# A hybrid decoder trunk on one core: the emission order recomputed from another table of durations, and some recurrent-branch operations moved to other engines

## The chip, the core and the metric

The program runs on one core of a Trainium2 chip. TensorE (PE in the profile) multiplies matrices into PSUM; VectorE (DVE), ScalarE (ACT) and GpSimd (POOL) work on tiles of 128 partitions; SyncE (SP), ACT and POOL issue transfers. Each engine runs its own instructions in program order and waits on semaphores of the others. The metric is the time of one execution on the device in microseconds; lower is better. The kernel before has a median of 2927.7 us over three runs, 2926.49 to 2927.87.

## The reference

Two layers over 512 tokens of width 1024, in float32. The middle part of a layer takes u = rmsnorm(x), one wide projection of u, and three branches that are gated, summed and projected back; a half-weighted SwiGLU stands ahead of it and behind it.

```python
for l in range(2):
    x = x + 0.5 * swiglu(rms_norm(x, ffn1_norm[l]), ...)      # 1024 -> 2 x 2816 -> 1024
    x = x + token_mixing(rms_norm(x, mix_norm[l]), ...)
    x = x + 0.5 * swiglu(rms_norm(x, ffn2_norm[l]), ...)
return rms_norm(x, final_norm)

# token_mixing, branch A (recurrent):
xa = causal_dwconv(rnn_x, conv_w) + conv_b                    # 4 taps
r, i = sigmoid(xa @ wa + ba), sigmoid(xa @ wx + bx)           # blocks of 64
log_a = -8 * r * softplus(-lam);  a = exp(log_a)
h = scan(a, sqrt(-expm1(2 * log_a)) * i * xa)                 # h_t = a_t h_{t-1} + u_t
ya = (h * gelu(rnn_g)) @ rnn_w_out
# branch B (short convolution):
yb = (c_b * causal_dwconv(c_c * c_h, sconv_w)) @ sconv_w_out  # 3 taps
# branch C: 8 heads attend, per query, to the 128 best keys of an indexer (8 heads of 64);
# merged = sum_b sigmoid(gate_b) * y_b ;  result = merged @ w_o
```

## The kernel before

Activations lie transposed: a tile is 128 channels by 512 tokens, so a vector of width 1024 is eight tiles (c or m from 0 to 7). Float32 accuracy comes from three products: every operand is cut into a high and a low part, and each product of a 128 by 128 weight tile with an activation tile is three matmuls of 512 columns (`mm3`, L528 to L530). I call these three one *tile product*; a *chunk* is the eight tile products that give one output tile in a PSUM bank of kind `psa`, of which there are three. Weights come in 512 KB pieces, one piece for eight tile products; in the middle part of a layer ACT makes high and negated low part (L378, L379) and a transfer that POOL issues adds the raw weight to the latter (L380). Three pairs of cut pieces are held.

What stands in which order on each engine is decided while the program is built. Each step of the computation is a Python generator that yields operations with a modelled cost (`PE`, `DVE`, `ACT`, `POOL` at L219 to L231). `Sched` plays them against a clock of its own: whenever an engine is free in the model, the ready operation of the lowest number is emitted to it (`_dispatch`). A step's number is its place in the program; `bump` makes evacuations of PSUM urgent (`EVAC`) and the top-k rounds of the indexer late (`TOPK_AT`). On the chip each engine then keeps exactly this order.

The change touches the middle part, `mix`. Its program in order of rank: v, indexer key and queries, k; then branch A. `a_x(c)` is the chunk x(c): DVE evacuates it into `xr` (L992), takes the first convolution tap (L994) and three more (L997); `cut` gives high part on ACT (L552) and low part on POOL (L556). `a_r(c)` makes two products of one tile each from it (ra, rx) with sigmoids on ACT (L1006, L1010). `a_scan` takes four channel tiles at a time: tanh, exp and square on ACT, two POOL operations in `em` (L1025, L1026), a square root on ACT, and in `fin` a multiply (L1036) and the scan (L1037) on DVE. `a_g(c)` is the gelu gate chunk g(c): evacuation (L1051), square on ACT, two POOL operations (L1054, L1055), tanh on ACT, two DVE operations (L1057 and, once the scan is there, L1059), and the cut into ya(c). Beside it `index(b)` scores the keys of query block b (L959 to L967) and finds the 128 best in 16 rounds of a maximum and a replacement (L971, L972; 48 rounds in a layer for the blocks of 256, 384 and 512 keys), with a threshold at the end (L974). `merge` then forms the sigmoid gates (chunks ga, evacuated at L1089) and the output projections of branch A (chunks wa(m), which need all eight ya). The attention heads q(h) follow, with `rope` (evacuation L855, shuffle L858, three POOL operations L859 to L861), then branch B, whose first tap is L1239, and w_o.

Of the kernel before, what the change touches and what calls it, by code (L numbers as in the profile page):

```python
# [15 lines left out]
AF = mybir.ActivationFunctionType  # L16
ALU = mybir.AluOpType
# [4 lines left out]
S = 512  # L22
# [99 lines left out]
class Sched:  # L122


    def __init__(self):
        self.t = 0.0
        self.n = 0
        self.heap = []
        self.free = {e: 0.0 for e in ("pe", "act", "dve", "pool", "sp")}
        self.ready = {e: [] for e in self.free}  # L130
        self.table = "sqrt"

    def _at(self, t, fn):
# [49 lines left out]
    def _dispatch(self):  # L183
        for eng, ready in self.ready.items():
# [17 lines left out]
            if s and self.table not in SETS[s]:  # L202
                self.table = SETS[s][0]
                cost += SWITCH
            op[3]()
            self.free[eng] = self.t + cost
# [14 lines left out]

def DVE(n, fn, fast=False, ap=0, **kw):
    return "dve", 0.07 + 0.06 * ap + n / (1920.0 if fast else 960.0), fn, kw


def ACT(n, fn, ap=0, **kw):
    return "act", 0.095 + 0.095 * ap + n / 1200.0, fn, kw


def POOL(n, fn, rate=0.0023, **kw):  # L230
    return "pool", 0.05 + n * rate, fn, kw  # L231

# [183 lines left out]
def trunk_kernel(ctx: ExitStack, tc: tile.TileContext, wall, wq, x_in, pos_in, cols_in, out):  # L416
# [37 lines left out]
    def col(name, l=0, j=0, c=0):  # L454
        i = col_of(name, l, j, c)
        return cols[:, i:i + 1]
# [408 lines left out]
    def mix(l, u, xs, nxt):  # L865
# [75 lines left out]
        def index(b, late):  # L941
# [27 lines left out]
            for rnd in range(TOPK // 8):  # L969
                m8 = sp.tile([P, 8], F32, name="m8", tag="m8", bufs=6)  # L970
                yield DVE(N, lambda: V.max(m8, acc[:, :N]), **bump)  # L971
                yield DVE(N, lambda: V.match_replace(out=acc[:, :N], in_to_replace=m8, in_values=acc[:, :N],  # L972
                                                     imm_value=-3e38), **bump)
            yield DVE(N, lambda: V.tensor_scalar(acc[:, :N], acc[:, :N], -2.9e38, NEG, op0=ALU.is_gt, op1=ALU.mult), True)  # L974
# [10 lines left out]
        def a_x(c):  # L985
# [7 lines left out]
            sch.release(banks["a"])  # L993
            yield DVE(S, lambda: V.tensor_scalar(y, xr[:, 0:S], col("rnn_conv_w", l, 0, c), col("rnn_conv_b", l, 0, c),  # L994
                                                 op0=ALU.mult, op1=ALU.add), True, ap=1)
            for j in range(1, 4):
# [18 lines left out]
        def a_scan(cs, pr):  # L1015
# [8 lines left out]
            def em(c, sq):  # L1024
                yield POOL(S, lambda: O.tensor_mul(sq, sq, th[c]))  # L1025
                yield POOL(S, lambda: O.tensor_add(th[c], th[c], sq))  # L1026

# [7 lines left out]
            def fin(c):  # L1035
                yield DVE(S, lambda: V.scalar_tensor_tensor(ix[c], th[c], 0.5, ix[c], op0=ALU.mult, op1=ALU.mult))  # L1036
                yield DVE(S, lambda: V.tensor_tensor_scan(th[c], rr[c], ix[c], 0.0, op0=ALU.mult, op1=ALU.add))  # L1037
                hs[c] = th[c]
                rr[c] = ix[c] = None
                sch.set(hev[c])  # L1040
# [6 lines left out]
        def a_g(c):  # L1047
# [5 lines left out]
            yield ACT(S, lambda: A.activation(t, g, AF.Square))  # L1053
            yield POOL(S, lambda: O.tensor_scalar(t, t, 0.044715 * GELU_C, GELU_C, op0=ALU.mult, op1=ALU.add), 0.00115)  # L1054
            yield POOL(S, lambda: O.tensor_mul(t, t, g))  # L1055
            yield ACT(S, lambda: A.activation(t, t, AF.Tanh), set="tanh")
            yield DVE(S, lambda: V.scalar_tensor_tensor(t, t, 1.0, g, op0=ALU.add, op1=ALU.mult))  # L1057
# [160 lines left out]
        def b_chunk(c):  # L1218
# [11 lines left out]
            def h_task():  # L1230
# [7 lines left out]
                y = box["y"] = G()  # L1238
                yield DVE(S, lambda: V.tensor_scalar(y, chb[:, 0:S], col("sconv_w", l, 0, c), None, op0=ALU.mult), True, ap=1)  # L1239
                for j in range(1, 3):  # L1240
# [187 lines left out]
```

## Time and profile before

| what | value |
|---|---|
| median of three runs | 2927.7 us |
| the profiled execution | 2929.0 us, its span 2927.3 us |
| TensorE busy in matmuls | 2857.4 us, 98% of the span |
| VectorE, ScalarE, GpSimd busy | 55%, 45%, 22% |
| mean granted TensorE clock | 0.987 |

The profile's page cuts the span into 40 slices of 73 us. VectorE stands at 9 tenths and more in two places, slices 7 and 8 (439 to 585 us, layer 0) and 27 and 28 (layer 1, 1448 us later), and the granted clock is at or above 9 tenths everywhere. The two places are branch A of each layer's middle part. A row of a windows view gives the busy time of each engine in a stretch, in brackets how many instructions reach into it, the mean granted clock, and the share of the transfer engines.

### The profile page before, as it was taken

The page shows a single profiled execution, that of the slowest core. Times are in us where ns is not written, and L with a number is a line of the kernel's source. Part 1 is how long each engine was busy: PE and PEld are TensorE (multiplying, and loading weights), DVE is VectorE, ACT ScalarE, POOL GpSimd, SP SyncE. Part 2 cuts the span into 40 slices and gives each one's busy share as a digit, 9 for nine tenths or more (in the row PEclk, how much of TensorE's full clock was granted, in tenths as well). Part 3 has the DMA queues.
Part 4 walks back from the last instruction along what each step waited for, and adds up shares of the span by engine and source line. Part 5 has one row for each costly group of instructions (what it writes and reads, how often), then busy time and mean ns, then how long its engine had stood idle before and what let it go on. Part 6 is the DMA issues. An engine that isn't in the chain of part 4 may idle for free.

```text
span 2927.3 us, 35856 instructions
## 1 busy us (share of the span) xinstructions
PE 2857.4 (98%) x14016; PEld 2384.6 (81%) x14016; DVE 1616.7 (55%) x2546; ACT 1319.5 (45%) x1817; POOL 638.5 (22%) x620
## 2 busy tenths in 40 slices
PE   8999998899999999999999999988999999999998
PEld 7888886678888888888888888866888888888887
DVE  7866659926312225666656666699171222256665
ACT  4333356647533453333433334566474334533333
POOL 1000064634222220000100001656242222300001
PEclk9999999899999999999999999999999999999999
DMA  4344486575688883344424444855846888733442
GB/s 165 106 115 112 134 188 143 136 165 136 140 189 187 190 189 94 105 116 114 129 85 112 114 111 141 192 136 133 180 119 152 197 185 186 180 85 114 112 117 63
DMA packets 118330, 407.47 MB, mean 139 GB/s; under 512 B 13137, under 2 KB 13777, under 8 KB 118161
## 3 DMA queue, kind: packets, MB, share of 16 engines
q1 hardware_dynamic: 77040, 263.23, 28.2%
q0 software_dynamic: 40400, 140.79, 27.5%
q8 instruction: 110, 1.80, 0.3%
q10 hardware_dynamic: 720, 1.17, 0.1%
q14 instruction: 60, 0.48, 0.1%
HBM read 281.40 MB, written 2.10 MB: 97 GB/s over the span
## 4 chain that ended last, share of the span: by engine, by line
PE 86%; DVE 11%; issue 1%; ACT 1%; DMA 0%; POOL 0%; SPq 0%; DVEq 0%; ACTq 0%; POOLq 0%
PE psa L530 23%; PE psa L529 23%; PE psa L528 23%; PE pst L722 2%; PE pst L719 2%; PE pst L721 2%; DVE g L972 2%; DVE m L971 2%; PE pso L721 1%; PE pso L722 1%; PE pso L719 1%; DVE g L997 1%; DVE g L965 1%; PE pss L719 1%; PE pss L722 1%
## 5 line engine op out<-in xcount | busy, mean ns | idle before, releaser
L528 PE MATMUL psa<-g,whi 128*128 128x512 f32 x3344 | 1332.6, 398 | 49.4 <-ACT g L552 17.2
L529 PE MATMUL psa<-g,whi 128*128 128x512 f32 x3344 | 1328.4, 397 | 4.6 <-POOL g L556 3.5
L530 PE MATMUL psa<-g,wlo 128*128 128x512 f32 x3344 | 1327.9, 397 | 1.2 <-DMA wlo<-wraw 1.2
L528 PEld LDWEIGHTS psa<-g,whi 128*128 128x128 f32 x3344 | 634.2, 190 | 194.8 <-issue 20.2
L530 PEld LDWEIGHTS psa<-g,wlo 128*128 128x128 f32 x3344 | 634.3, 190 | 151.3 <-DMA wlo<-wraw 2.1
L529 PEld LDWEIGHTS psa<-g,whi 128*128 128x128 f32 x3344 | 634.0, 190 | 146.7 <-POOL g L556 5.2
L384 ACT CAST whi<-wraw 128x768 fp32r<-128x768 f32 (+1 forms) x359 | 339.2, 950 | 764.3 <-PE pst L721 232.6
L378 ACT ACTIVATE wlo<-wraw 128x1024 fp32r<-128x1024 f32 x232 | 245.7, 1059 | 534.3 <-PE psa L530 526.5
L385 DVE TENSOR_TENSOR wlo<-wraw,whi 128x768 fp32r<-128x768 f32 (+1 forms) x359 | 391.6, 1101 | 31.8 <-ACT whi L384 27.1
L380 POOL DMA_DIRECT2D wlo<-wraw x232 | 201.3, 868 | 525.5 <-ACT wlo L378 498.7
L379 ACT CAST whi<-wraw 128x1024 fp32r<-128x1024 f32 x232 | 239.5, 1032 | 0.0
L722 PE MATMUL pst<-g,wlo 128*128 128x256 f32 x576 | 162.0, 281 | 0.6 <-DVE wlo L385 0.5
L721 PE MATMUL pst<-g,whi 128*128 128x256 f32 x576 | 161.7, 281 | 0.0
L719 PE MATMUL pst<-g,whi 128*128 128x256 f32 x576 | 161.6, 281 | 0.0
L317 POOL DMA_DIRECT2D wraw<-in_wq_dram x24 | 20.9, 872 | 625.9 <-DMA wraw<-in_wq_dram 469.9
L782 DVE SCALAR_TENSOR_TENSOR x<-pst,x 128x512 f32<-128x512 f32 x96 | 66.4, 692 | 149.0 <-PE pst L722 148.6
L336 POOL DMA_DIRECT2D wraw<-in_wq_dram x24 | 20.9, 871 | 548.6 <-DVE wlo L385 509.4
L719 PEld LDWEIGHTS pst<-g,whi 128*128 128x128 f32 x576 | 108.5, 188 | 4.3
L721 PEld LDWEIGHTS pst<-g,whi 128*128 128x128 f32 x576 | 108.4, 188 | 4.2
L722 PEld LDWEIGHTS pst<-g,wlo 128*128 128x128 f32 x576 | 108.6, 188 | 1.0 <-DVE wlo L385 1.0
L598 POOL TENSOR_TENSOR g<-g 128x512 f32<-128x512 f32 x44 | 61.0, 1387 | 216.6 <-ACT g L589 216.4
L1089 DVE TENSOR_TENSOR g<-psa,g 128x512 f32<-128x512 f32 x48 | 33.1, 689 | 133.7 <-PE psa L530 125.3
(219 smaller groups left out, 3167.1 us busy)
## 6 DMA issues: line engine op xcount, KB each, us to landing
wraw<-in_w_dram SPq DMA_DIRECT2D x423, 512.0 KB, 4.0
wlo<-wraw POOLq DMA_DIRECT2D x232, 512.0 KB, 5.6
wraw<-in_wq_dram SPq DMA_DIRECT2D x96, 384.0 KB, 3.0
wraw<-in_wq_dram POOLq DMA_DIRECT2D x48, 384.0 KB, 4.9
x<-in_x_dram SPq DMA_DIRECT2D x8, 256.0 KB, 4.4
out_dram<-g ACTq DMA_DIRECT2D x4, 256.0 KB, 3.0
out_dram<-g SPq DMA_DIRECT2D x4, 256.0 KB, 3.3
wraw<-in_w_dram SPq DMA_DIRECT2D x4, 128.0 KB, 4.2
```

The lines of the kernel that those rows point to most:

```text
L378: yield ACT(u.w, lambda: A.mul(u.lo, u.raw, -1.0))
L379: yield ACT(u.w, lambda: A.copy(u.hi, u.raw))
L380: yield "pool", 0.9, lambda: O.dma_start(u.lo, u.raw, accum_op=ALU.add), {}
L384: yield ACT(u.w, lambda: A.copy(u.hi, u.raw))
L385: yield DVE(u.w, lambda: V.tensor_sub(u.lo, u.raw, u.hi.bitcast(F32)), ap=1)
L528: T.matmul(ps, wh, xh, start=first, stop=False)
L529: T.matmul(ps, wh, xl, start=False, stop=False)
L530: T.matmul(ps, wl, xh, start=False, stop=last)
L719: T.matmul(o, u.hi[:, c], xh, start=begin and k == 0 and m == 0, stop=False, skip_group_check=True)
L721: T.matmul(o, u.hi[:, c], xl, start=False, stop=False, skip_group_check=True)
L722: T.matmul(o, u.lo[:, c], xh, start=False, stop=k == n - 1 and m == 1, skip_group_check=True)
L782: return DVE(S, lambda: V.scalar_tensor_tensor(dst, src, f, dst, op0=ALU.mult, op1=ALU.add), ap=1, **kw)
```

## The change

The model learns three things: an operation on DVE waits in the model for the POOL operation in progress (`port`; top-k rounds and PSUM evacuations are exempt, as are POOL operations of up to 8 elements), the top-k operations have a higher cost, and so has the scan. The computation changes in four places: `em` becomes one DVE operation, th * (sq + 1), in the place of two on POOL; the inner polynomial of gelu becomes one DVE operation in the place of two on POOL, its factor moved into the scale of the tanh; the first taps of both convolutions move from DVE to ACT. Lines behind L205 shift by 8 and less.

```diff
+        self.port = 0.0
...
+            if op[4].get("port"):
+                if eng == "dve":
+                    cost += max(0.0, self.port - self.t)
+                else:
+                    self.port = self.t + 0.85 * cost
...
 def DVE(n, fn, fast=False, ap=0, **kw):
+    kw.setdefault("port", "bump" not in kw)
...
 def POOL(n, fn, rate=0.0023, **kw):
+    kw["port"] = n > 8
...
-                yield DVE(N, lambda: V.max(m8, acc[:, :N]), **bump)
+                yield DVE(N, lambda: V.max(m8, acc[:, :N]), ap=2, **bump)
...
-                                                     imm_value=-3e38), **bump)
+                                                     imm_value=-3e38), ap=3, **bump)
...
-            yield DVE(S, lambda: V.tensor_scalar(y, xr[:, 0:S], col("rnn_conv_w", l, 0, c), col("rnn_conv_b", l, 0, c),
-                                                 op0=ALU.mult, op1=ALU.add), True, ap=1)
+            yield ACT(S, lambda: A.activation(y, xr[:, 0:S], AF.Identity, scale=col("rnn_conv_w", l, 0, c),
+                                              bias=col("rnn_conv_b", l, 0, c)), ap=1)
...
-                yield POOL(S, lambda: O.tensor_mul(sq, sq, th[c]))
-                yield POOL(S, lambda: O.tensor_add(th[c], th[c], sq))
+                yield DVE(S, lambda: V.scalar_tensor_tensor(th[c], sq, 1.0, th[c], op0=ALU.add, op1=ALU.mult))
...
-                yield DVE(S, lambda: V.tensor_tensor_scan(th[c], rr[c], ix[c], 0.0, op0=ALU.mult, op1=ALU.add))
+                yield DVE(S, lambda: V.tensor_tensor_scan(th[c], rr[c], ix[c], 0.0, op0=ALU.mult, op1=ALU.add), ap=9)
...
-            yield POOL(S, lambda: O.tensor_scalar(t, t, 0.044715 * GELU_C, GELU_C, op0=ALU.mult, op1=ALU.add), 0.00115)
-            yield POOL(S, lambda: O.tensor_mul(t, t, g))
-            yield ACT(S, lambda: A.activation(t, t, AF.Tanh), set="tanh")
+            yield DVE(S, lambda: V.scalar_tensor_tensor(t, t, 1.0 / 0.044715, g, op0=ALU.add, op1=ALU.mult))
+            yield ACT(S, lambda: A.activation(t, t, AF.Tanh, scale=0.044715 * GELU_C), set="tanh")
...
-                yield DVE(S, lambda: V.tensor_scalar(y, chb[:, 0:S], col("sconv_w", l, 0, c), None, op0=ALU.mult), True, ap=1)
+                yield ACT(S, lambda: A.activation(y, chb[:, 0:S], AF.Copy, scale=col("sconv_w", l, 0, c)), ap=1)
```

What this does to the order is seen at two places of layer 0. The first is VectorE at the end of branch A, before the change. `g_110` holds the scores of the block of 512 keys, L974 is its threshold, L1036, L1037 and L1059 end channel tiles 4 to 7 of the branch, L1089 evacuates gates.

```order
L971 MAX m8_4958<-g_110 128x8
L972 MATCH_REPLACE g_110<-m8_4958,g_110 128x512
L974 TENSOR_SCALAR g_110<-g_110 128x512
L1089 TENSOR_TENSOR g_4976<-psa_4922,g_3456 128x512
L1057 SCALAR_TENSOR_TENSOR g_4921<-g_4921,g_4920 128x512
L1089 TENSOR_TENSOR g_5022<-psa_4977,g_3456 128x512
L1036 SCALAR_TENSOR_TENSOR g_4613<-g_4851,g_4613 128x512
L1037 SCALAR_TENSOR_TENSOR g_4851<-g_4554,g_4613 128x512
L1059 TENSOR_TENSOR g_4715<-g_4715,g_4851 128x512
```

The same place after it; L1065 is the former L1059, L863 and L866 are the evacuation and shuffle of heads q0 and q1, L979 and L980 the former L971 and L972.

```order
L1065 TENSOR_TENSOR g_4722<-g_4722,g_4839 128x512
L1044 SCALAR_TENSOR_TENSOR g_4840<-g_4680,g_4741 128x512
L1044 SCALAR_TENSOR_TENSOR g_4841<-g_4762,g_4814 128x512
L1065 TENSOR_TENSOR g_4787<-g_4787,g_4840 128x512
L863 TENSOR_TENSOR g_5091<-psa_5049,g_3456 128x512
L1065 TENSOR_TENSOR g_4851<-g_4851,g_4841 128x512
L866 STREAM_SHUFFLE g_5092<-g_5091 32x512
L980 MATCH_REPLACE g_110<-m8_4991,g_110 128x512
L979 MAX m8_5126<-g_110 128x8
L980 MATCH_REPLACE g_110<-m8_5126,g_110 128x512
L979 MAX m8_5139<-g_110 128x8
```

Before, all 48 top-k rounds and the last threshold stand ahead of the last four L1059; now a replacement and 14 whole rounds over 512 keys, and that threshold, stand behind the last L1065, among the evacuations of wa(0) to wa(2). Between the chunk g(7) and the first tile product of wa(0) PE has 34 tile products before (gates ga(0) to ga(3) and two of q(0)) and 50 now (the same gates, q(0), q(1) and two of q(2)).

The second place is GpSimd ahead of the same four multiplies, before the change. L1025 and L1026 are `em` for tiles 4 to 7.

```order
L1055 TENSOR_TENSOR g_4921<-g_4921,g_4920 128x512
L1025 TENSOR_TENSOR g_4933<-g_4933,g_4851 128x512
L1025 TENSOR_TENSOR g_4972<-g_4972,g_4852 128x512
L380 DMA wlo_4982<-wraw_4617 128x1024
L1026 TENSOR_TENSOR g_4851<-g_4851,g_4933 128x512
L1026 TENSOR_TENSOR g_4852<-g_4852,g_4972 128x512
L1025 TENSOR_TENSOR g_4985<-g_4985,g_4853 128x512
L1025 TENSOR_TENSOR g_5012<-g_5012,g_4854 128x512
L1026 TENSOR_TENSOR g_4853<-g_4853,g_4985 128x512
```

And after it; L1020 is the former L1012, the product of gate and input for tile 7, L564 the cut of ya, L867 the first POOL operation of the rope of q(0).

```order
L1020 TENSOR_TENSOR g_4814<-g_4814,g_4586 128x512
L388 DMA wlo_4857<-wraw_4502 128x1024
L388 DMA wlo_4907<-wraw_4569 128x1024
L388 DMA wlo_4960<-wraw_4613 128x1024
L388 DMA wlo_5008<-wraw_4667 128x1024
L564 TENSOR_TENSOR g_5037<-g_4661,g_5036 128x512
L388 DMA wlo_5054<-wraw_4716 128x1024
L564 TENSOR_TENSOR g_5069<-g_4722,g_5068 128x512
L867 TENSOR_TENSOR g_5093<-g_5091,cq_88 32x512
```

The seven `em` operations that stood close together are gone from GpSimd, and the rope of a head now stands between two cuts of ya. Over the whole program ScalarE has 43 table loads in the new order and 35 in the old one; the eight more stand with the sigmoids of the gates and the exponentials of the heads. PE's order outside the middle parts of the layers is the same.

## Rows read from the trace of the kernel before

**Rows 1.** Head of the page: busy us, share of the span, instructions.
```profile
PE 2857.4 (98%) x14016; PEld 2384.6 (81%) x14016; DVE 1616.7 (55%) x2546; ACT 1319.5 (45%) x1817; POOL 638.5 (22%) x620
```
**Rows 2.** Who waited for whom, on PE: total us, times, longest.
```profile
PE psa L528 <- ACT g L552: 17.2, 4, 7.3
PE psa L528 <- DVE xr L992: 14.5, 4, 6.0
PE psa L528 <- DVE g L1089: 9.5, 4, 4.1
```
**Rows 3.** Windows of branch A, both layers: busy time of each engine.
```profile
core 0: us, PE busy (x) PEld busy (x) DVE busy (x) ACT busy (x) POOL busy (x), PEclk, DMA share, GB/s
482.00:500.00 18.00, 17.45 (x74) 13.82 (x74) 17.10 (x50) 12.62 (x18) 6.86 (x8) 1.00 0.58 147
500.00:536.00 36.00, 20.94 (x67) 15.36 (x68) 34.77 (x51) 23.13 (x30) 25.18 (x24) 0.81 0.53 132
536.00:580.00 44.00, 41.94 (x173) 32.93 (x171) 42.94 (x72) 33.83 (x46) 27.65 (x27) 0.96 0.60 132
580.00:602.00 22.00, 15.51 (x54) 11.43 (x55) 18.62 (x18) 11.77 (x17) 13.48 (x10) 0.89 0.57 138
602.00:662.00 60.00, 60.00 (x249) 48.34 (x249) 9.04 (x14) 23.80 (x27) 13.29 (x14) 0.96 0.81 179
...
1948.00:1984.00 36.00, 20.33 (x67) 15.11 (x68) 35.12 (x51) 23.30 (x30) 25.15 (x24) 0.80 0.55 131
```
**Rows 4.** A window of branch B, where PE never waits.
```profile
820.00:900.00 80.00, 80.00 (x345) 64.63 (x345) 17.74 (x26) 30.38 (x32) 19.94 (x24) 1.00 0.86 190
```
**Rows 5.** Groups of VectorE instructions, 482 to 602 us: busy us, mean ns.
```profile
L1036 DVE SCALAR_TENSOR_TENSOR g<-g 128x512 f32<-128x512 f32 x8 | 8.4, 1051 | 0.0
L1059 DVE TENSOR_TENSOR g<-g 128x512 f32<-128x512 f32 x8 | 8.4, 1050 | 0.1
L1057 DVE SCALAR_TENSOR_TENSOR g<-g 128x512 f32<-128x512 f32 x7 | 7.3, 1045 | 0.0
L994 DVE TENSOR_SCALAR g<-xr,cols 128x512 f32<-128x512 f32 x4 | 6.1, 1535 | 0.6 <-DVE xr L992 0.5
```
**Rows 6.** VectorE in order of time: start us, us.
```profile
571.55 1.72 DVE L1057 SCALAR_TENSOR_TENSOR g<-g 128x512 f32<-128x512 f32 x1
573.19 0.68 DVE L971 MAX8 m<-g 128x8 f32<-128x512 f32 x1
...
574.70 7.08 DVE L974 TENSOR_SCALAR g<-g 128x512 f32<-128x512 f32 x1
581.70 0.68 DVE L1089 TENSOR_TENSOR g<-psa,g 128x512 f32<-128x512 f32 x1
582.30 0.68 DVE L1057 SCALAR_TENSOR_TENSOR g<-g 128x512 f32<-128x512 f32 x1
```
**Rows 7.** GpSimd in the same stretch.
```profile
571.42 3.01 POOL L1025 TENSOR_TENSOR g<-g 128x512 f32<-128x512 f32 x2
...
575.01 2.81 POOL L1026 TENSOR_TENSOR g<-g 128x512 f32<-128x512 f32 x2
577.52 2.75 POOL L1025 TENSOR_TENSOR g<-g 128x512 f32<-128x512 f32 x2
579.99 1.50 POOL L1026 TENSOR_TENSOR g<-g 128x512 f32<-128x512 f32 x1
```
**Rows 8.** One line of VectorE over the run: ns least, median, most.
```profile
L997 DVE SCALAR_TENSOR_TENSOR g<-xr,cols,g x48: 721/752/1822, 435.3 to 1988.2; 128x512 f32<-128x512 f32 x48
```
**Rows 9.** Groups of ScalarE instructions, 482 to 602 us.
```profile
L1021 ACT ACTIVATE g<-g,spp 128x512 f32<-128x512 f32 x8 | 5.3, 709 | 0.0
L1032 ACT ACTIVATE g<-g 128x512 f32<-128x512 f32 x8 | 5.0, 624 | 0.1
L1044 ACT ACT_TABLE_LOAD x3 | 3.8, 1283 | 0.1
```

## The prediction

> **What bounds the kernel now.** I read the head of the page first. PE is in matmuls for 98% of the span, DVE for only 55% [rows 1], so nothing that merely relieves DVE on average is worth anything; what counts is where PE does not run at its full rate. The view of waits on PE names three large items: a tile that ACT cuts (L552), an evacuation of `xr` and one of a gate, 41.2 us in twelve waits over both layers [rows 2]. They lie in branch A, so I read that stretch by windows [rows 3], beside a window of branch B in which PE never waits [rows 4].
>
> A window tells what was lost as follows. In branch B 345 matmuls of 512 columns fill 80 us, 0.232 us each, 0.696 us for a tile product [rows 4]. From 482 to 662 us the five windows hold 74, 67, 173, 54 and 249 matmuls, which at that rate would cover 17.2, 15.5, 40.1, 12.5 and 57.7 us; the windows are 18, 36, 44, 22 and 60 us long. The losses are 0.8, 20.5, 3.9, 9.5 and 2.3 us, together 36.9 us [rows 3]. That is more than the idle time, since the granted clock falls to 0.81 and 0.89 behind the long waits, parts of these stretches being run at 1.2 GHz in the place of 2.4. Matmuls on a border are counted twice, so it is 1 or 2 us more. Layer 1 repeats it (36 us with 67 matmuls again), so 74 us in all are lost in the two branches A. With all of it back, the profiled execution would fall from 2929.0 to 2855 us. Start and end of the program stay as they are.
>
> In the same stretch DVE is busy for 17.10, 34.77, 42.94 and 18.62 of 120 us, 113.4 us [rows 3]. Between the chunk g(3) and the first of wa PE has 80 tile products of the branch and 34 of filler, 114, which take 79.3 us at the full rate. So DVE has 34.1 us more to do than PE there, and PE lost 36.9. It is DVE's stage, and I use the ratio 36.9 / 34.1 = 1.08 below for what an overhang of DVE costs with its lower clock.
>
> **The change part by part.** I add up what DVE must have done by the last multiply that ends a ya (L1059), from the 113.4 us, for layer 0.
>
> The deferred top-k. One round over 512 keys takes 1.51 us from the start of its maximum to the start of what follows (573.19 to 574.70) [rows 6]. A replacement and 14 rounds, 14.5 rounds, go behind the branch: 21.9 us less. They land in the stretch of wa, where DVE was busy for 9.04 of 60 us [rows 3]; the evacuations of wa stand among them, each at most one round late, and three PSUM banks give two chunks of 5.6 us to cover that. First user of the result is the softmax of the heads, which PE meets after more than ten chunks.
>
> The last threshold (L974). It took 7.08 us, from 574.70 to 581.78 [rows 6], while POOL ran one `em` operation after another until 581.49 [rows 7]; an ordinary DVE operation of 512 columns takes 0.68. The gate's evacuation behind it is one of the three waits of PE [rows 2]. It goes behind the branch with its rounds, and the `em` operations that held it up leave POOL: 7.1 us less.
>
> The first taps. Four L994 in the stretch took 6.1 us [rows 5]; they go. On ACT one costs 0.624 us without and 0.709 with one per-partition operand [rows 9], so 0.79 with two as an estimate; 0.62 and 0.90 are the bounds. That is 3.2 us more in 120 of which ACT is busy for 81 [rows 3]. The tap now waits on ACT for DVE's evacuation, and behind it in ACT's queue stand the cuts of the weight pieces; with three pieces held, of 5.6 us of PE each, 11 us cover that, and if the cover went, PE would wait for weights by as much as the evacuation is late. In branch B the tap leaves a DVE that is busy for 17.74 of 80 us for an ACT that is busy for 30.38, beside a PE that is busy throughout [rows 4]: nothing. Eight more table loads of 1.283 us [rows 9] are 10.3 us of ACT over the run, in stretches like 602 to 662, where it is busy for 23.80 of 60 [rows 3]: nothing.
>
> The operations that come from POOL. Eight for `em` and seven for gelu in this stretch. L1057 has the very form, two inputs of 512 columns from SBUF; undisturbed one such operation starts 0.60 us after the one ahead of it (581.70 to 582.30) [rows 6]. 15 times 0.60 is 9.0 us more.
>
> The waits on POOL. L1036, L1059 and L1057 average 1.05 us [rows 5] against 0.68 undisturbed [rows 6]: 0.37 times 23, 8.5 us of waiting. POOL's operations with two inputs in branch A go from 48 per layer (16 cuts, 8 products in L1012, 16 in `em`, 8 in gelu) to 24. I take half of the wait per instruction: 4.2 us less for these 23, and 15 times 0.185, 2.8 us, more for the new ones. The bounds for the new ones are no wait and 1.04 us each (the 1.72 of 571.55 less 0.68 [rows 6]), 0 and 15.6 us.
>
> Sum: 113.4 - 21.9 - 7.1 - 6.1 + 9.0 - 4.2 + 2.8 = 85.9 us. PE's filler ahead of wa grows by 16 tile products to 50, so that it has 130, 90.4 us. DVE now fits, with 4.5 us to spare. What stays lost I put at 5 us per layer: the 0.8 and 2.3 us of the two outer windows, and 2 us for waits of half a microsecond at single products, since the order is fixed and DVE's spare time is small. So 36.9 - 5 = 31.9 us per layer come back, 63.8 in all: 2929.0 - 63.8 = 2865.2 for the profiled execution. The median stands 1.3 us below that execution, so I say 2864.
>
> The Trainium skill (SBUF — State Buffer, "Who interferes with whom") says that a DVE operation in a two-port mode, or with two SBUF inputs, and a GpSimd operation take turns at a shared port, each for one whole instruction. The trace agrees for L1057 at 571.55, which took one POOL operation more than its own time, and not for L974, which outlasted five. By that rule the moved threshold would be worth the 1.5 us of one POOL operation and not 7.1 less its own time; the sum would be 5 us higher per layer for DVE, which the spare 4.5 us nearly hold, and the time 2866.
>
> **The rivals.** *The new operations wait.* Each of the 15 meets a POOL operation in progress and waits 1.04 us. For it: the means of L1036 and L1059 are half as long again as their own time, so about every third one waited that long [rows 5, 6]. Against it: POOL has half as many such operations, and 48 L997 have a median of 752 ns beside a least of 721 [rows 8]. DVE then has 85.9 + 15.6 - 2.8 = 98.7 us, 8.3 over PE; with the ratio 9.0, and with the 5 us of before 14.0 lost per layer. 2929.0 - 2 x 22.9 = 2883, a median of 2882. The Trainium skill (Perfetto Trace Analysis, "Optimizing Scalar/DVE Operations") speaks on this side: the two engines share a port, so that moving operations between them may not help.
>
> *Starving behind POOL (slower).* L974 shows that a DVE operation can stand behind a whole row of POOL operations, 6.4 us above 0.68 [rows 6, 7]. The ya cuts on POOL now have the rope of a head among them, and the DVE operations beside them are those that wa waits for. If such rows catch DVE often, each time costs 6.4 us. It decides from six times per layer: 85.9 + 6 x 6.4 = 124.3 is 34 us above PE's 90.4, the overhang of now. At eight times it is 137.1, 46.7 over, 50.4 lost with the ratio: 2929.0 + 2 x 13.5 = 2956, a median of 2955. Against it: the long wait was one threshold in each layer, none of the 48 L997 took over 1.82 us [rows 8], and the row of `em` that made it is gone.
>
> *It is not DVE's stage (no change).* PE could be waiting for weights, whose transfers POOL issues, and DVE's work be a coincidence; then 36.9 us stay lost and the median stays at 2928. For it: the transfer engines are at 0.81 and 0.86 when PE runs without waiting [rows 3, 4]. Against it: they are at 0.53 to 0.60 where PE waits, and the waits name ACT and DVE [rows 2].
>
> **How the numbers follow.** The forecast has 70%, with a range of its own from 2852 to 2878 (nothing lost, or 12 us per layer). The waiting operations have 17%, no change 5%, starving 7%; 1% is left for more than the counted loss coming back. A measurement of this kernel can tell about 0.2%, 6 us, from no change. Faster: 70 + 17 + 1 = 88%; same 5%; slower 7%. The range goes from 2850 (all of it back, with the matmuls on the borders) to 2896, which takes in the waiting operations up to 21 us lost per layer; outside lie no change, starving, and some 6% of the rest.
>
> **What would show it.** In windows of the same length from g(3) on, PE should hold some 155 matmuls in 36 us at a granted clock of 1.00, and DVE should be near 9 tenths of them. The last threshold should take under 3 us and start after the first evacuation of wa. L1043, L1065 and L1061 should average under 0.9 us; the waits of PE on L1095 and on `xr` L1000 should be below 2 us each per layer, and the wait of ra on ACT's cut below 2. Between 602 and 662 DVE should rise from 9 to above 30 us with PE still full. The prediction is wrong if the clock still falls below 0.95 in branch A, if wa still waits on ya by more than 5 us, or if PE waits for ACT's first tap or for weights.

## The result and the profile after

The changed kernel takes 2856.81 us (median of four runs, 2856.48 to 2857.57) against 2927.78 for the kernel before on the same chip (2926.49 to 2928.44). The ratio is 0.9758, with an interval from 0.9742 to 0.9775. The profiled execution took 2857.57 us; its mean granted clock is 0.997, against 0.987. The forecast was 2864, inside a range from 2850 to 2896.

The head of the page, which answers to [rows 1]:

```profile
span 2855.8 us, 35874 instructions
PE 2829.6 (99%) x14016; PEld 2371.4 (83%) x14016; DVE 1583.7 (55%) x2546; ACT 1347.6 (47%) x1857; POOL 562.4 (20%) x556
```

The number of matmuls is the same, and VectorE is as busy on average as before. Next the waits on PE, which answer to [rows 2] (what was waited for, us in total, times, longest):

```profile
PE psa L536 <- ACT whi L381: 5.3, 1, 5.3
PE psa L536 <- ACT g L1018: 2.8, 2, 1.4
PE pss L1157 <- DVE g L562: 2.2, 2, 1.2
...
PE psa L536 <- DVE xr L1000: 0.3, 2, 0.2
```

The first line is the start of the program, which nothing here touches. Of the three waits that cost 41.2 us, the one on `xr` is left with 0.3 us, and the ones on ACT's cut (L552, now L560) and on the gate's evacuation are gone. One product of the branch now waits 1.4 us in each layer for a sigmoid on ACT (L1018). Windows of branch A, as in [rows 3]; the last one lies in branch A of layer 1:

```profile
480.56:570.63 90.07, 88.52 (x380) 70.99 (x379) 87.45 (x153) 78.04 (x105) 35.67 (x34) 1.00 0.77 178
500.00:536.00 36.00, 34.45 (x148) 27.27 (x147) 35.62 (x47) 28.77 (x41) 23.94 (x20) 1.00 0.77 173
580.00:602.00 22.00, 20.78 (x97) 17.11 (x96) 19.86 (x53) 13.70 (x23) 6.08 (x6) 1.00 0.80 181
602.00:662.00 60.00, 60.00 (x278) 49.36 (x277) 17.68 (x45) 35.27 (x52) 12.81 (x13) 1.00 0.77 178
1930.00:1966.00 36.00, 34.62 (x149) 27.95 (x150) 35.13 (x69) 29.28 (x42) 15.06 (x14) 1.00 0.75 174
```

In 36 us there are now 148 matmuls (layer 1: 149) where 67 stood in either layer, and the granted clock is 1.00 where it was 0.81 and 0.80. (The page of the kernel before has 8 tenths in slice 8, which holds most of that stretch; that the clock stood at 9 tenths and more everywhere, as said above, was not so.) The first row runs from the start of g(3) to the end of the last multiply that ends a ya. DVE is busy for 87.45 us of it; the chunk of wa(0) starts at 573.20, so PE took 92.6 us from g(3) to it. DVE's rows for the same stretch answer to [rows 5] (busy us, mean ns of one, idle before them):

```profile
L979 DVE MAX8 m<-g 128x8 f32<-128x384 f32 (+2 forms) x26 | 13.7, 526 | 0.4
L1005 DVE SCALAR_TENSOR_TENSOR g<-xr,cols,g 128x512 f32<-128x512 f32 x12 | 13.4, 1113 | 0.5 <-ACT g L1002 0.2
L1044 DVE TENSOR_TENSOR_SCAN g<-g 128x512 f32<-128x512 f32 x8 | 12.6, 1593 | 0.0
L1043 DVE SCALAR_TENSOR_TENSOR g<-g 128x512 f32<-128x512 f32 x8 | 6.4, 811 | 0.6 <-ACT g L1051 0.6
L1065 DVE TENSOR_TENSOR g<-g 128x512 f32<-128x512 f32 x8 | 6.4, 806 | 0.0
L1033 DVE SCALAR_TENSOR_TENSOR g<-g 128x512 f32<-128x512 f32 x8 | 5.4, 686 | 0.3 <-ACT g L1039 0.2
L1063 DVE SCALAR_TENSOR_TENSOR g<-g 128x512 f32<-128x512 f32 x7 | 5.4, 770 | 0.0
L1061 DVE SCALAR_TENSOR_TENSOR g<-g 128x512 f32<-128x512 f32 x6 | 5.2, 874 | 0.0
```

L1033 and L1061 are the operations that came from POOL. The three products that averaged 1.05 us are at 0.77 to 0.81 us; but the later taps and the scan, which no term of the sum names, have become dearer: between 480 and 600 us the kernel before has `L997 ... x12 | 9.9, 824` and `L1037 ... x8 | 9.8, 1220`, against 1113 and 1593 ns here.

Where the time came from can be told more closely. For each kernel I take a window's length less the columns of the matmuls that start in it at the full rate (0.2323 us for 512 columns); what is left is lost. The second column group shows the evacuation of x(4), the first chunk for the second half of the recurrent channels, and when its last tap ended (us from the span's start, layer 0). Each ratio is to runs of the kernel before on the same chip at the same time (medians of 2926.4 to 2927.8 us), so differences of a few us between two kernels are to be read with the intervals.

| kernel | median, us | ratio to before (interval) | lost 500–540 | lost 540–620 | x(4): evacuated, taps end |
|---|---|---|---|---|---|
| before | 2927.8 | – | 21.9 | 14.7 | 505.4, 510.1 |
| order by the new costs, old operations (e1) | 2886.7 | 0.9861 (0.9845–0.9878) | 11.2 | 9.1 | 493.8, 504.9 |
| new operations, old costs (e2) | 2894.2 | 0.9886 (0.9871–0.9901) | 12.6 | 8.1 | 499.7, 505.0 |
| cost of top-k alone (e3) | 2906.6 | 0.993 (0.991–0.995) | 17.9 | 9.7 | 498.1, 504.1 |
| the port alone (e4) | 2898.7 | 0.9903 (0.9883–0.9923) | 15.6 | 9.0 | 498.5, 507.6 |
| threshold with two inputs (e5) | 2924.8 | 0.9991 (0.998–1.0002) | 22.1 | 14.3 | – |
| half the top-k rounds (e9) | 2897.6 | 0.9897 (0.9868–0.9925) | 14.7 | 8.4 | 491.0, 499.1 |
| order by new costs, late `em` (e13) | 2893.1 | 0.9885 (0.9867–0.9903) | 7.7 | 14.1 | 494.2, 497.9 |
| the change | 2856.8 | 0.9758 (0.9742–0.9775) | 1.9 | 1.6 | 491.9, 497.0 |
| the change, maximum twice (e10) | 2901.4 | 0.991 (0.9881–0.9938) | 10.7 | 14.5 | 498.8, 504.0 |
| the change, first taps on DVE (e7) | 2861.2 | 0.9772 (0.9744–0.9801) | 6.1 | 0.5 | 490.4, 494.1 |
| the change, gelu on POOL (e8) | 2861.5 | 0.9777 (0.9759–0.9795) | 2.1 | 4.7 | 491.4, 496.7 |
| the change, `em` on POOL (e11) | 2869.3 | 0.9803 (0.9785–0.9821) | 4.7 | 7.5 | 494.7, 500.6 |
| the change, dearer taps (e12) | 2852.4 | 0.9745 (0.9732–0.9758) | 2.6 | 0.3 | 490.6, 495.9 |

### The profile page after: what moved, and what is told of

Read it like the earlier page. It is cut to its first block, busy times and chain, and to the rows that moved or that the text cites. A ratio compares the mean times of both kernels' runs of the same rounds, so it can differ in the third digit from the quotient of the medians.

```text
span 2855.8 us, 35874 instructions
## 1 busy us (share of the span) xinstructions
PE 2829.6 (99%) x14016; PEld 2371.4 (83%) x14016; DVE 1583.7 (55%) x2546; ACT 1347.6 (47%) x1857; POOL 562.4 (20%) x556
## 4 chain that ended last, share of the span: by engine, by line
PE 91%; DVE 6%; ACT 2%; issue 1%; DMA 0%; SPq 0%; DVEq 0%; ACTq 0%
PE psa L536 24%; PE psa L538 24%; PE psa L537 24%; PE pst L730 2%; PE pst L727 2%; PE pst L729 2%; PE pso L727 1%; PE pso L730 1%; PE pso L729 1%; DVE g L1044 1%; DVE g L1005 1%; DVE g L980 1%; PE pst L1187 1%; PE pss L727 1%; PE pss L729 1%
## 5 line engine op out<-in xcount | busy, mean ns | idle before, releaser
L388 POOL DMA_DIRECT2D wlo<-wraw x232 | 200.8, 866 | 569.1 <-ACT wlo L386 549.7
L767 DVE TENSOR_TENSOR g<-psa,g 128x512 f32<-128x512 f32 x88 | 60.8, 691 | 77.4 <-PE psa L538 77.3
```

What stands on the lines that cost most here:

```text
L388: yield "pool", 0.9, lambda: O.dma_start(u.lo, u.raw, accum_op=ALU.add), {}
```

## The experiments

Three theories stood at the start. The balance (T1): DVE's work up to the last ya against PE's products, whatever the order. The order (T2): the new order does it, the operations do nothing. The port (T3): the operations that leave POOL do it by relieving DVE of waits.

**Order alone and operations alone.** e1 has the changed costs and the old operations (the port's factor is 0.6; its order comes out of the model with the old operations, so it is not the change's order row by row). e2 has the new operations and the old costs.

```diff
 e1:
+                    self.port = self.t + 0.6 * cost
+                yield DVE(N, lambda: V.max(m8, acc[:, :N]), ap=2, **bump)
...
+                yield DVE(S, lambda: V.tensor_tensor_scan(...), ap=9)
 e2:
+            yield ACT(S, lambda: A.activation(y, xr[:, 0:S], AF.Identity, ...), ap=1)
+                yield DVE(S, lambda: V.scalar_tensor_tensor(th[c], sq, 1.0, th[c], op0=ALU.add, op1=ALU.mult))
+            yield DVE(S, lambda: V.scalar_tensor_tensor(t, t, 1.0 / 0.044715, g, op0=ALU.add, op1=ALU.mult))
```

> The model's new costs alone (port, top-k, scan), operations as before; the port factor is 0.6 in the place of 0.85. Its order puts 10.5 top-k rounds and the last threshold behind the last ya and gives PE 50 tile products of filler. Theory 1 (what counts is DVE's work ahead of the last ya against PE's products): DVE 113.4 - 15.9 - 7.1 = 90.4 us against 90.4 of PE, about 5 us lost per layer, 2864. Theory 2 (the order alone counts, being nearer to what the chip does): the same, 2857 to 2864. Theory 3 (the work taken off GpSimd frees the shared port, the order hardly matters): most of the loss stays, 2905 to 2925.

> The moved operations alone, under the old costs. No top-k round goes behind the last ya, filler 42 products. Theory 1: DVE 113.4 - 6.1 (taps) - 6.4 (threshold no longer behind em) + 9.0 - 4.2 + 2.8 = 108.5 us against 122 products, 84.9 us; 23.6 over, times 1.08 is 25.5 lost per layer, 2905. Theory 2: near 2925. Theory 3: 2857 to 2870.

Measured: 2886.7 and 2894.2 us, so 41 and 34 us of the 71; together a little more than the whole. T2 and T3 alone fall. T1 missed both: it expected 2864 of e1, nearly all of the gain, and 2905 of e2. In e1 PE waits at xr:

```profile
PE psa L536 <- DVE xr L1000: 13.9, 4, 6.1
```

DVE in that stretch of e1 (start us, us, instruction):

```profile
493.84 0.68 DVE L1000 TENSOR_TENSOR xr<-psa,g 128x512 f32<-128x512 f32 x1
494.63 7.42 DVE L1002 TENSOR_SCALAR g<-xr,cols 128x512 f32<-128x512 f32 x1
502.08 0.75 DVE L1005 SCALAR_TENSOR_TENSOR g<-xr,cols,g 128x512 f32<-128x512 f32 x1
```

and POOL beside it (L1033 and L1034 are `em` in e1, L388 issues a transfer):

```profile
494.56 0.86 POOL L388 DMA_DIRECT2D wlo<-wraw  x1
495.18 2.81 POOL L1034 TENSOR_TENSOR g<-g 128x512 f32<-128x512 f32 x2
...
497.72 2.80 POOL L1033 TENSOR_TENSOR g<-g 128x512 f32<-128x512 f32 x2
500.22 1.53 POOL L1034 TENSOR_TENSOR g<-g 128x512 f32<-128x512 f32 x1
501.45 1.13 POOL L388 DMA_DIRECT2D wlo<-wraw  x1
```

The first tap of x(4) stands 7.42 us in DVE, until the row of five `em` operations is through: what befell the threshold in the kernel before [rows 6, 7] befalls a tap here. It is earlier in branch A and so delays ra(4) to ra(7) and all behind them. From this came a fourth theory, that of the *nearer deadline*: not DVE's sum up to the last ya decides, but when the chunks x(4) to x(7) are evacuated and convolved. The runs below support it in part; none moves the evacuation of x(4) and nothing else. In the kernel before, the last matmul of x(4) is this one on PE:

```profile
493.17 0.39 PE L530 MATMUL psa<-g,wlo 128*128 128x512 f32 x1
```

and DVE comes to its evacuation (L992) 11.8 us later, since the old order has 25 top-k rounds ahead of it:

```profile
504.94 0.54 DVE L972 MATCH_REPLACE8 g<-m,g 128x384 f32<-128x384 f32 x1
505.40 0.68 DVE L992 TENSOR_TENSOR xr<-psa,g 128x512 f32<-128x512 f32 x1
506.19 1.04 DVE L994 TENSOR_SCALAR g<-xr,cols 128x512 f32<-128x512 f32 x1
```

The change has 15 ahead of it, and the chunk, which ends at 491.9, is evacuated at once; its three later taps end at 497.0:

```profile
491.95 0.68 DVE L1000 TENSOR_TENSOR xr<-psa,g 128x512 f32<-128x512 f32 x1
492.55 0.68 DVE L1033 SCALAR_TENSOR_TENSOR g<-g 128x512 f32<-128x512 f32 x1
...
494.67 2.33 DVE L1005 SCALAR_TENSOR_TENSOR g<-xr,cols,g 128x512 f32<-128x512 f32 x3 [0.24 <-ACT g L1002]
```

**The parts of the costs.** e3 has the dearer top-k and nothing else of the change, e4 the port and nothing else.

```diff
 e3:
+                yield DVE(N, lambda: V.max(m8, acc[:, :N]), ap=2, **bump)
+                yield DVE(N, lambda: V.match_replace(...), ap=3, **bump)
 e4:
+                    cost += max(0.0, self.port - self.t)
+                else:
+                    self.port = self.t + 0.85 * cost
```

> Only the higher modelled cost of the top-k operations. 5 rounds and the threshold go behind the last ya, filler 42. Theory 1: 113.4 - 7.6 - 7.1 = 98.7 us against 84.9, 13.8 over, 14.9 lost per layer, 2884. Theory 2: between 2870 and 2890, as the largest error of the model is mended. Theory 3: no change, 2920 or more.

> Only the modelled port. 1.5 rounds and the threshold go behind the last ya, filler 50. Theory 1: 113.4 - 2.3 - 7.1 = 104.0 us against 90.4, 13.6 over, 14.7 lost per layer, 2883. Theory 2: between 2880 and 2905. Theory 3: no change, 2920 or more.

2906.6 and 2898.7: each helps by 21 and 29 us, less than the balance gives for the rounds that they defer (2884 and 2883). The order alone (T2) had 2870 to 2890 and 2880 to 2905, so only e4 lies in its range. In both, x(4) is evacuated near 498, later than in e1.

**What kind of operation waits.** In e5 the last threshold of layer 0 is a two-input operation in the place of L974.

```diff
+                yield DVE(N, lambda: V.scalar_tensor_tensor(acc[:, :N], acc[:, :N], -2.9e38, neg1.to_broadcast([P, N]),
+                                                            op0=ALU.is_gt, op1=ALU.mult), True)
```

> The kernel before, with the three top-k thresholds of layer 0 as a scalar_tensor_tensor with a broadcast second input from SBUF, in the place of a tensor_scalar; layer 1 unchanged, as a control; order and instruction count the same. If the long wait belongs to the kind of operation (a tensor_scalar cannot get in between two GpSimd operations, one with two inputs can), the last threshold of layer 0 takes at most 2.4 us, layer 1's still 7, PE's wait for the gate shrinks from 4.1 to under 1 us in layer 0, and the time falls by 4 to 6 us to 2922 to 2924. If any DVE operation would stand behind the whole row, it takes 6 to 7 us in both layers and the time stays at 2928.

```profile
573.50 7.35 DVE L977 SCALAR_TENSOR_TENSOR g<-g,neg 128x512 f32<-128x512 f32 x1
```

By the first answer it would have taken at most 2.4 us, and it took 7.35: of these two forms of a DVE operation neither is spared the long wait. The time didn't move beyond the noise (0.998 to 1.0002).

**Less and more top-k.** e9 is the kernel before with every second top-k round left out; e10 is the change with each maximum taken twice.

```diff
 e9:
+                yield DVE(N, lambda: rnd % 2 or V.max(m8, acc[:, :N]), **bump)
+                yield DVE(N, lambda: rnd % 2 or V.match_replace(out=acc[:, :N], ...), **bump)
 e10:
+                yield DVE(N, lambda: (V.max(m8, acc[:, :N]), V.max(m8, acc[:, :N])), ap=2, **bump)
```

> The kernel before with every second top-k round left out (24 of 48 per layer, so that 64 and not 128 keys are chosen), the order of everything else as before. Theory 1: 53 us of rounds in the stretch from g(3) on become 26.5, DVE 86.9 us against 79.3 of PE, 7.6 over, 8.2 lost per layer and 2 to 5 of small waits, 2870 to 2876. Theory 2 (the order must be mended): 2905 or more. Theory 3 (the port): 2905 or more, since no operation with two inputs goes.

> The changed kernel with the maximum of every top-k round done twice on DVE, which the model doesn't know of; order and result the same. From g(3) to the last ya that is 25.5 more maxima, 14 us (8 x 0.46, 16 x 0.58, 1.5 x 0.71). Theory 1: DVE's 90 us become 104 against PE's 92.6 in that stretch, 11.5 over, about 12 lost per layer, 2880 to 2884. If DVE had more to spare than the sum says, 2860 to 2870; if each late operation is paid by PE in full (17 us with the 8 maxima ahead of g(3)), 2890 or more.

By the balance, e9 has so much taken from DVE that 10 to 13 us per layer should stay lost (2870 to 2876). It took 2897.6, under the 2905 of the other two theories as well, and still waits for `xr`:

```profile
PE psa L528 <- DVE xr L992: 16.3, 4, 4.2
```

There x(4) is evacuated on time, at 491.0, but its taps end only 8 us later, two of them taking 5.06 us together from 492.77 on, while POOL ran `em`. That is the strongest evidence against the balance alone: the work is gone and the time is not back. In e10 the order is the change's but the rounds ahead of x(4) last longer, and its evacuation falls to 498.8; it gives back 44.6 of the 71 us. That is the third answer of the expectation (2890 or more) and not the 2880 to 2884 of the balance, and at 22 us per layer it is more than the 17 us of maxima that were added.

**Each operation by itself, in the change.** The factor of the port is another one in two of them (0.9 in e7, 0.8 in e11), so a part of the difference can be the order's.

```diff
 e7:
+            yield DVE(S, lambda: V.tensor_scalar(y, xr[:, 0:S], col("rnn_conv_w", l, 0, c), ...), True, ap=1)
 e8:
+            yield POOL(S, lambda: O.tensor_scalar(t, t, 0.044715 * GELU_C, GELU_C, op0=ALU.mult, op1=ALU.add), 0.00115)
+            yield POOL(S, lambda: O.tensor_mul(t, t, g))
 e11:
+                yield POOL(S, lambda: O.tensor_mul(sq, sq, th[c]))
+                yield POOL(S, lambda: O.tensor_add(th[c], th[c], sq))
```

> The changed kernel with the first tap of the recurrent branch back on DVE (four in the stretch), known to the model; its port factor is 0.9 in the place of 0.85. 14.5 rounds and the threshold still behind the last ya, filler 50. By the term of the sum (6.1 us): DVE 96 against 92.6, 3.7 lost per layer, 2864. If the taps' waits were owed to em on GpSimd, which is gone: 4 x 0.55 = 2.2 us more, 2857 to 2859.

> The changed kernel with gelu's two operations back on GpSimd, known to the model. 12 rounds behind the last ya, 17 top-k rounds ahead of the evacuation of x(4). The runs so far say that two things are lost in x(4) to x(7): evacuations that stand behind too many rounds, and taps on DVE that wait for em on GpSimd. Gelu's operations stand beside the g chunks and not there: 2858 to 2864. If any operation with two inputs on GpSimd costs alike, they are half of what came off it: 2872 or more.

> The changed kernel with em's two operations back on GpSimd, known to the model (port factor 0.8). 13.5 rounds behind the last ya, 16.5 ahead of x(4). If em beside the taps of x(4) to x(7) is the costly meeting: the taps of x(4) or x(5) end 4 to 6 us later than in the changed kernel, 6 to 10 us more are lost per layer between 500 and 540 us, 2868 to 2878. If all operations on GpSimd cost alike: the same as with gelu there, within 4 us.

2861.2, 2861.5 and 2869.3: over the change's 2856.8 the taps of branch A on ACT make 4.4 us, gelu 4.7 and `em` 12.5. The intervals of the first two ratios overlap that of the change, so that neither is shown to be worth anything; that of `em` doesn't (from 0.9785 up, against 0.9775 at most). So `em` is the one part of the three that counts clear of noise, though it puts work on DVE. The taps came out between their two answers, and gelu in the first of its own. e11 lies in the range of its first answer (2868 to 2878), but not by the meeting named there: the taps of x(4) end 3.6 us later and not 4 to 6, and of what is lost beside the change 2.8 us lie between 500 and 540, where 6 to 10 were expected, and 5.9 behind that.

**Out of the taps' way.** e13 is e1 with `em` of the first four tiles held until x(7) is convolved, so that no row of `em` can meet a tap of x(4) to x(7); factor 0.5.

```diff
+                if c < 4:
+                    yield xa[7].ev
```

> The model's new costs alone with the old operations (port factor 0.5), and em of the tiles 0 to 3 made to wait until x(7) is cut. 20 rounds ahead of x(4), 3 rounds and no less behind the last ya. If em beside the taps is what the new order alone could not mend: at most 5 us lost between 500 and 540 us, against 11.2 with em in its place, and the tap of x(4) ends within 6 us of its evacuation; the whole 2868 to 2882, since the later em now meets the rounds. If the place of em is of no account: 10 us or more still lost there, 2884 or more.

Half of it came true. The taps of x(4) end 3.7 us after its evacuation (11 in e1), and the loss from 500 to 540 falls from 11.2 to 7.7 us, where at most 5 were expected. But the total is 2893.1, above e1 and above the expected 2868 to 2882, in the range of the other answer (2884 or more). The row of `em` met another victim, the threshold of 384 keys on DVE:

```profile
526.18 9.07 DVE L982 TENSOR_SCALAR g<-g 128x384 f32<-128x384 f32 x1
```

while POOL ran `em` (L1035 and L1036 in e13) without a pause:

```profile
525.76 0.88 POOL L388 DMA_DIRECT2D wlo<-wraw  x1 [0.35 <-ACT wlo L386]
526.37 1.59 POOL L1035 TENSOR_TENSOR g<-g 128x512 f32<-128x512 f32 x1
527.61 4.04 POOL L1036 TENSOR_TENSOR g<-g 128x512 f32<-128x512 f32 x3
531.31 1.16 POOL L388 DMA_DIRECT2D wlo<-wraw  x1
531.92 1.88 POOL L1036 TENSOR_TENSOR g<-g 128x512 f32<-128x512 f32 x1
533.17 1.85 POOL L1020 TENSOR_TENSOR g<-g 128x512 f32<-128x512 f32 x1
```

PE's largest wait in e13 is then one for DVE:

```profile
PE psa L536 <- DVE g L1061: 7.5, 2, 3.8
```

In layer 0 it lasts from 535.1 to 538.8; the threshold ends at 535.25, and two rounds stand between it and that evacuation. That the one makes the other is read from the times and was not tried by itself. The taps of x(4) are one victim of the rows among several: the change takes the row off POOL, while moving it in time moved the damage.

**Dearer taps in the costs.** Since a tap takes 752 ns in the median (1113 on average in the stretch above, waits included) and the model gives it about 0.66 us (0.07 + 0.06 + 512/960), e12 raises their cost in the change, with the port's factor at 0.7.

```diff
+                    self.port = self.t + 0.7 * cost
...
+                                                            op0=ALU.mult, op1=ALU.add), ap=2)
```

> The changed kernel with a modelled cost of the taps on DVE of 0.72 in the place of 0.66 us (the trace has 0.74), port factor 0.7: an attempt on the rest, 1.4 us of wait at ra(6) and 1.2 at a head per layer. If a nearer table still helps, 2850 to 2855; if the rest is the program's own chain of operations, no change within 0.1%.

2852.38 us (2851.63 to 2852.7, five runs), ratio 0.9745 (0.9732 to 0.9758): the best median of all, and in the range that was expected if a nearer table still helps. By the medians it is 4.4 us below the change, by the ratios 4; the intervals of the two ratios overlap, and the two did not run beside each other, so that it beats the kernel before for certain, while a gain over the change is likely and not shown. The wait of the heads on L562, 2.2 us in the change, is not among its waits on PE, and the one on the sigmoid (L1018) stands at 2.8 us as in the change.

**DVE's time as it was.** T1 has two halves: DVE's sum up to the last ya, and the time that follows from it by the ratio 1.08. The traces tell them apart. The rows run from the start of g(3) to the end of the last multiply that ends a ya, for the kernel before, e1, e3, e4, e9 and e10 in this order (columns as in [rows 3], DVE's time the third of the five):

```profile
482.00:598.23 116.23, 94.26 (x363) 72.60 (x363) 112.83 (x188) 77.57 (x104) 71.03 (x63) 0.91 0.57 136
480.53:582.72 102.19, 94.31 (x387) 74.61 (x386) 99.10 (x152) 73.75 (x98) 68.42 (x61) 0.95 0.69 163
480.69:591.41 110.72, 93.06 (x368) 71.41 (x367) 108.22 (x173) 77.61 (x103) 71.52 (x64) 0.94 0.60 143
479.21:587.76 108.55, 98.52 (x393) 77.15 (x392) 105.29 (x176) 74.20 (x99) 69.26 (x64) 0.94 0.69 159
479.62:581.53 101.91, 89.21 (x364) 69.83 (x362) 89.23 (x116) 75.18 (x101) 69.59 (x62) 0.95 0.66 156
480.14:586.96 106.82, 97.46 (x393) 76.61 (x392) 103.38 (x191) 79.19 (x106) 34.25 (x34) 0.95 0.64 152
```

In e1 and e3 the sum was mis-sized: DVE is busy for 99.10 and 108.22 us where T1 had 90.4 and 98.7, for the most part since a row of POOL had caught another operation (the tap of 7.42 us in e1). In e3 that was a product of the gelu branch:

```profile
564.87 8.93 DVE L1057 SCALAR_TENSOR_TENSOR g<-g 128x512 f32<-128x512 f32 x1
```

With the measured sums T1's own reckoning, (99.10 - 90.4) x 1.08 + 5 and (108.22 - 84.9) x 1.08 us lost per layer, gives about 2884 and 2905, beside the 2886.7 and 2906.6 of the runs, so these two don't speak against the balance. In e4, e9 and e10 the sum is within 2.4 us of the expected one (104.0, 86.9 and 104), and the time lies some 11 to 20 us above what the ratio makes of it. In e9 DVE is idle for 12.7 of 101.91 us while PE loses time; in e10 a head waits 5.3 us per layer for a cut on DVE (L562), behind the last ya, where the sum doesn't reach. So the balance is a part of the account and not the whole.

## Why the prediction was right, and where its reasons were not

*Branch A loses 36.9 us per layer, and this can come back: right.* The profiled execution fell by 2929.0 - 2857.57 = 71.4 us, 35.7 per layer. With it the rival by which it is not DVE's stage (2928) is gone: the transfer engines stand at 0.77 in the windows above, under the 0.81 and 0.86 that they had before where PE was full [rows 3, 4], and PE is full.

*DVE's sum: right, some terms by luck.* 85.9 us were forecast up to the last ya, 87.45 measured. The rounds did go behind: the last threshold (L982) starts at 600.35, nearly 19 us after the first evacuation of wa (L1107, at 581.6), and takes 0.43 us:

```profile
600.35 0.43 DVE L982 TENSOR_SCALAR g<-g 128x512 f32<-128x512 f32 x1
```

The tap on ACT was put at 0.79 and took 0.813. The port's term was wrong in its place. Waits on POOL were to halve everywhere (4.2 us less, 2.8 more). The three products lost more than that: 1.05 to about 0.80, 0.25 on each of 23, 5.8 us. But the taps gained 0.29 us on each of 12 and the scan 0.37 on each of 8, 6.4 us, and the new operations stand between the 0.686 of `em` and the 0.874 of gelu. Of the eight scans three take 2.16 to 2.25 us, each begun while POOL was at a cut (L564), and the others 1.21 to 1.23. Waiting was not halved but found at other operations, and that the total came out right, since the two nearly cancel, is luck.

*What stays lost: 5 us were too many, by the totals.* By the prediction's own count it is 36.9 - 35.7 = 1.2 us per layer. Twice the difference is the 7.6 us between the forecast 2865.2 and the 2857.57 of the profiled execution. Counted directly, 1.9 + 1.6 = 3.5 us stay lost between 500 and 620 where 36.6 were, so that some 2.6 us per layer came back outside these 120 us.

*The marks.* 155 matmuls in 36 us at 1.00: 148. DVE near 9 tenths: 35.62 of 36, still more. L1043 and L1065 and L1061 under 0.9 us: 0.81, 0.81, 0.87. Waits on `xr` and on L1095 under 2 us per layer: 0.15 and none. One mark was wrong: between 602 and 662 DVE was to rise from 9 to above 30 us, and stands at 17.68. The window had been laid by the times of the kernel before. Branch A now ends earlier, so that the deferred rounds fill 580 to 602 (19.86 of 22) and are over at 600.8.

*The step that doesn't hold in general is the one that turns DVE's overhang into time: "DVE has 34.1 us more to do than PE there, and PE lost 36.9. It is DVE's stage".* From two numbers close to each other the prediction took a ratio of 1.08. The forecast did not have to lean on it, since in the change DVE's sum falls below what PE has (87.45 against 92.6 us). Where an overhang is left, the ratio came out in e1 and e3, with DVE's time as it was, and not in e4, e9 and e10. e9 takes half of the top-k away, its sum is as expected, and 23 of 36.6 us of loss between 500 and 620 stay. That DVE looks full tells little by itself: it is busy for 38.77 and 39.49 of the 40 us from 500 to 540 before and after, with 21.9 and 1.9 us lost.

What decides beside the sum is in part argued. PE needs x(4) to x(7) evacuated and convolved by the time it gets to ra(4). Before, two things stood in the way: 25 rounds of a maximum and a replacement ahead of the evacuation, which the order mends, and rows of `em` on POOL behind which a DVE operation stands, which the operations mend. Each alone leaves the other: 41 and 34 us of 71. But e13, where the taps are on time, loses less between 500 and 540 and more behind that (14.1 us against 9.1 in e1), so the nearer deadline doesn't decide alone either. The prediction knew of the rows from the threshold, priced them there at 7.1 us, and did not ask which operation a row would catch in another order.

*The rivals.* The new operations did not each wait 1.04 us (they take 0.69 and 0.87 us with all waits). Starving behind POOL came in the runs that keep `em` on POOL in its rows (e1 7.42 us, e3 8.93, e4 5.54, e9 7.46, e13 9.07), and not in the change, since its row of `em` is gone, as the prediction argued. (In e11, with `em` back on POOL in the new order, no DVE operation of layer 0 took over 2.8 us.) The Trainium skill (SBUF — State Buffer, "Who interferes with whom") has the shared port taken for one instruction at a time. The threshold of e5 and the tap of e1 outlasted four and more POOL operations, so here too the trace does not agree. The Trainium skill (Perfetto Trace Analysis, "Optimizing Scalar/DVE Operations") has it that moving operations between the two may not help; here `em` on DVE is worth 12.5 us, and gelu's 4.7 are within the noise.

*What stays open.* Why a DVE operation sometimes waits for one POOL operation and sometimes for a whole row. Of the seven long waits of layer 0, those of the kernel before, e1, e5, e9 and e13 began within half a microsecond of the start of a POOL transfer issue, with two-input operations queued behind it without a gap. That the issue opens the wait is not borne out by the other two: in e3 the issue had begun 0.94 us earlier and `em` was running, and in e4 the tap began 1.97 us after the start of the issue, in the second `em` operation of a row:

```profile
499.25 5.54 DVE L1002 TENSOR_SCALAR g<-xr,cols 128x512 f32<-128x512 f32 x1
497.28 0.87 POOL L388 DMA_DIRECT2D wlo<-wraw  x1
497.92 2.80 POOL L1034 TENSOR_TENSOR g<-g 128x512 f32<-128x512 f32 x2
```

Why e4, e9 and e10 lose more than DVE's sum gives is open too.

## What to carry to other kernels

A sum of an engine's work against its consumer's is not enough (e9): check it again at the earlier products that the consumer meets in that stretch, in the order that the engine will really keep, and count in the sum what the engine may wait for, since such a wait comes back at another operation in another order (e1, e3). A planner's table nearer to the times traced helped here (e3: 21 us), and so did a planner that knows who blocks whom (e4: 29 us). When an operation that another engine waits for is caught by a row of work elsewhere, take the row away; here shifting it in time found the next victim (e13).

## What the runs showed of the hardware

A DVE operation on SBUF data can stand behind a row of back-to-back GpSimd operations for 7.08 (before), 7.35 (e5), 7.42 (e1), 7.46 (e9), 8.93 (e3) and 9.07 us (e13), against 0.43 for the same threshold of 512 keys with POOL out of the way. It happened to operations with one SBUF input of full width (before, e1, e13) as to those with two (e3, e5, e9). When the row was cut, waits were found elsewhere: the scan rose from 1220 to 1593 ns on average, while the products beside it fell from 1.05 to 0.80 us.
